# Two-layer mixer with mixture-of-experts: the first experts' biases as two-part float32r rows, and their gate applied to the experts' rows

## The chip, the cores and the metric

The kernel runs on one core of a Trainium2 chip. The metric is the device time of one execution in microseconds (us); lower is better. The time before is 2146.15 us, the median of three runs (2144.57 to 2146.51).

## The reference, cut to what matters

The program is two whole blocks, one after the other, over 256 tokens of width 1024 in float32. Only the feed-forward part of the first block is touched: 32 experts, of which every token uses four.

```python
def moe_ffn(h, w_router, b_router, w_gate_up, b_gate_up, w_down, b_down):
    ...
    top_val, top_idx = lax.top_k(logits, TOP_K)          # TOP_K = 4 of 32
    probs = jax.nn.softmax(top_val, axis=-1)
    ...
    def expert_block(args):
        xb, e = args
        gu = xb @ w_gate_up[e] + b_gate_up[e]            # 1024 -> 2048
        x_glu = jnp.minimum(gu[:, 0::2], SWIGLU_LIMIT)
        x_lin = jnp.clip(gu[:, 1::2], -SWIGLU_LIMIT, SWIGLU_LIMIT)
        act = x_glu * jax.nn.sigmoid(SWIGLU_ALPHA * x_glu) * (x_lin + 1)
        return act @ w_down[e] + b_down[e]               # 1024 -> 1024
    ...
    out = jnp.einsum('tk,tkd->td', probs.astype(y_pairs.dtype), y_pairs)
```

The block then adds `gate * out` to the residual `x`, where `gate` is one row of 1024 numbers that comes from the conditioning vector and is the same for all tokens.

## The kernel before, in words

`moe1` computes these experts, one after another, over 64 slots each. For each group of four experts, `gather` picks the tokens' columns with one-hot products into `gT`. Per expert, `expert1a` makes the gate-and-up product: eight weight tiles `w` (128 x 2048 float32, 1024 KB) stream through TensorE against the slots of `gT`. Since there are only 64 slots, the output is folded: the two halves `s` of the columns stand on partitions 0 to 63 and 64 to 127 of two accumulators `gu` (128 x 512), so each product writes 64 rows. The bias is added by more products (`brows`, L1332), and VectorE and ScalarE make `act` from it. `expert1b` transposes `act` (`aT`), spreads the one-hots (`oT`), streams four tiles of the down weights into one folded accumulator `y`, adds its bias, and calls `combine`: `weighted` multiplies `y` by the routing weights and splits the result into two float32r parts (`yhi` on ScalarE, `ylo` on VectorE), eight products with `oT` scatter them back to the 256 tokens (`co`, four accumulators of 128 x 512), and VectorE multiplies each by the gate (`gated`, L1193) and adds it to `x` (L1194).

The lambda `pend` delays `expert1b` of expert e until after `expert1a` of expert e+1, and a scheduler then moves instructions a little on each engine. After expert 11 comes `overflow`, a branch for experts with more than 64 tokens: every engine and the DMA queue pass it together. Nine tiles of expert 12 are issued ahead of it, one into the spare slot and eight into `w2`.

The weights arrive through one DMA queue, issued by SyncE (SP) in the order gate-and-up of e+1, then down of e, at L302, into 14 slots that are used in turn: five of the whole program (`own`), one spare, eight of this stage. An issue waits until TensorE has read the tile that was in its slot. The second block (`block2`) loads its first weights into the five `own` slots.

The bias of expert e enters as a product whose stationary operand is a column of the identity, broadcast: it picks row e of a 32-row table.

```python
nc.tensor.matmul(o, pick(r, j).to_broadcast([32, 64]), brows[r, c:c + 512], start=False, stop=True)
```

Of the kernel before, what the change touches and what calls it, by code (L numbers as in the profile page):

```python
# [7 lines left out]
F32 = mybir.dt.float32  # L8
F32R = mybir.dt.float32r
# [4 lines left out]
OP = mybir.AluOpType  # L14
# [216 lines left out]
class Ker:  # L231
# [65 lines left out]
    def wload(self, src, n=WCOL, slot=None):  # L297
        pool, tag = slot or self.wq[self.wi % len(self.wq)]
        t = pool.tile([128, WCOL], F32, name="w", tag=tag, bufs=None)
        if slot is None:  # L300
            self.wi += 1
        self.nc.sync.dma_start(t[:, :n], src)  # L302
        return t
# [873 lines left out]
        nc.vector.scalar_tensor_tensor(lo, y, w, hi.bitcast(F32), op0=OP.mult, op1=OP.subtract)  # L1177
        return hi, lo

    def combine(self, p, x, y, oT, w, gate, bufs=1):  # L1180

        nc = self.nc
        ys = self.weighted(p, y, w, bufs)
        for b in range(2):
            o = [self.ps("co"), self.ps("co")]
            for i in range(2):
                for s in range(2):
                    nc.tensor.matmul(o[s], oT[64 * s:64 * s + 64, 128 * b:128 * b + 128], ys[i][64 * s:64 * s + 64, :],  # L1188
                                     start=(i == 0), stop=(i == 1))
            for s in range(2):  # L1190
                cs = slice(512 * s, 512 * s + 512)
                part = p.tile([128, 512], F32, name="gated", tag="gated", bufs=1)
                nc.vector.tensor_mul(part, o[s], gate[:, cs])  # L1193
                nc.vector.tensor_add(x[:, b, cs], x[:, b, cs], part)  # L1194

    def spread(self, p, ohv, bufs=1):
# [55 lines left out]
    def expert1a(self, p, g, c0, wload, bias, feed=iter(())):  # L1252

        nc = self.nc
        gu = [self.pg("gu"), self.pg("gu")]
        for k in range(8):
            if k % 2 == 0:
                next(feed, None)
            w = wload(k)
            for j in range(2):  # L1260
                for s in range(2):
                    nc.tensor.matmul(gu[j][64 * s:64 * s + 64, :], g[:, k, c0:c0 + 64],  # L1262
                                     w[:, 1024 * s + 512 * j:1024 * s + 512 * j + 512], start=(k == 0), stop=False)
        for j in range(2):
            for s in range(2):
                bias(gu[j][64 * s:64 * s + 64, :], 0, 1024 * s + 512 * j)
        act = p.tile([128, 512], F32, name="act", tag="act", bufs=2)
        lin = p.tile([128, 512], F32, name="lin", tag="lin", bufs=1)
        sg = p.tile([128, 512], F32, name="sge", tag="sge", bufs=1)
        for j in range(2):  # L1270
            cs = slice(256 * j, 256 * j + 256)
            nc.vector.tensor_scalar(act[:, cs], gu[j][:, 0::2], 7.0, None, op0=OP.min)  # L1272
            nc.vector.tensor_scalar(lin[:, cs], gu[j][:, 1::2], 7.0, -7.0, op0=OP.min, op1=OP.max)
        self.last_sig = nc.scalar.activation(sg, act, AF.Sigmoid, scale=1.702)  # L1274
        nc.vector.tensor_mul(act, act, sg)
        nc.vector.scalar_tensor_tensor(act, lin, 1.0, act, op0=OP.add, op1=OP.mult)
        return act

    def expert1b(self, p, x, act, wload, bias, ohv, wv, gate):
        nc = self.nc  # L1280
        pt = self.ps("aT")
        for j in range(4):
            nc.tensor.transpose(pt[:, 128 * j:128 * j + 128], act[:, 128 * j:128 * j + 128], self.ident)
        aT = p.tile([128, 4, 2, 64], F32, name="aT", tag="aT", bufs=1)
        nc.scalar.copy(aT.rearrange("p j s n -> p (j s n)"), pt)
        oT = self.spread(p, ohv)
        y = self.ps("y")
        for k in range(8):
            if k % 2 == 0:
                w = wload(8 + k // 2)  # L1290
            for s in range(2):
                o = 1024 * (k % 2) + 512 * s
                nc.tensor.matmul(y[64 * s:64 * s + 64, :], aT[:, k % 4, k // 4, :], w[:, o:o + 512], start=(k == 0), stop=False)  # L1293
        for s in range(2):
            bias(y[64 * s:64 * s + 64, :], 1, 512 * s)
        self.combine(p, x, y, oT, wv, gate)

    def moe1(self, p, route, ahead, spare):
        nc, d, tc = self.nc, self.d, self.tc
        A, B = self.Affn, self.mcol1[:, 0, 24:32]  # L1300
        x = self.x1
        sel, cw, r = route

        def fetch(e, j, slot=None):
            if isinstance(e, int):
                gu, dn = d['wgu'][e], d['wdn'][e]
            else:
                gu = d['wgu'][bass.ds(e, 1)].rearrange("e k n -> (e k) n")
                dn = d['wdn'][bass.ds(e, 1)].rearrange("e k n -> (e k) n")
            if j < 8:  # L1310
                return self.wload(gu[128 * j:128 * j + 128, :], slot=slot)
            return self.wload(dn[128 * (j - 8):128 * (j - 8) + 128, :], slot=slot)
        first = {(0, j): fetch(0, j, ahead) for j in range(NW2)}
        self.wi = 0
        brows = p.tile([96, 1024], F32, name="brows")
        for j in range(2):
            nc.sync.dma_start(brows[32 * j:32 * j + 32, :], d['bgu'][:, 1024 * j:1024 * j + 1024])
        nc.sync.dma_start(brows[64:96, :], d['bdn'])
        self.load_gf()
        gtb = p.tile([128, 1024], F32, name="gtb2")  # L1320
        self.bcast_rows([(1, 10), (1, 11)], [gtb[:, 0:512], gtb[:, 512:1024]])
        xs = self.split_tokens(p, x, r)
        pm, cnt = self.slots(p, sel)

        def wl(e):
            return lambda j: first.pop((e, j)) if isinstance(e, int) and (e, j) in first else fetch(e, j)

        def bias_of(pick):
            def bias(o, which, c):
                j, c = (2, c) if which else divmod(c, 1024)  # L1330
                r = slice(32 * j, 32 * j + 32)
                nc.tensor.matmul(o, pick(r, j).to_broadcast([32, 64]), brows[r, c:c + 512], start=False, stop=True)  # L1332
            return bias

        def late(g, c0, i, ohv, w):
            bsel = p.tile([96, 1], F32, name="bsel")
            for j in range(3):
                r = slice(32 * j, 32 * j + 32)
                nc.vector.tensor_copy(bsel[r, :], self.ident[r, 32 * j:32 * j + 32][:, bass.ds(i, 1)])
            bias = bias_of(lambda r, j: bsel[r, 0:1])  # L1340
            self.expert1b(p, x, self.expert1a(p, g, c0, wl(i), bias), wl(i), bias, ohv, w, gtb)
        pend = None
        for e in range(32):
            feed = iter(())
            if e % 4 == 0:
                oh = self.onehots(p, pm, e)
                g, feed = self.gather(p, xs, 4, [oh[:, b].rearrange("p e s -> p (e s)") for b in range(2)], A, B)
                next(feed)
                if pend:
                    pend()  # L1350
                    pend = None
            bias = bias_of(lambda r, j, e=e: self.ident[r, 32 * j + e:32 * j + e + 1])
            act = self.expert1a(p, g, 64 * (e % 4), wl(e), bias, feed)
            if e == 0:
                cw = cw()
            if e % 4 == 0:
                sw = self.slot_weights(p, [(slice(64 * s, 64 * s + 64), j, [oh[:, b, j, :] for b in range(2)],
                                            [cw[:, b, e + j:e + j + 1] for b in range(2)]) for j in range(4) for s in range(2)], "sw", 4)
            if pend:
                pend()  # L1360
            ohv = [oh[:, b, e % 4, :] for b in range(2)]
            pend = lambda act=act, e=e, ohv=ohv, bias=bias, w=sw[:, e % 4:e % 4 + 1]: self.expert1b(p, x, act, wl(e), bias, ohv, w, gtb)
            if e == OVF:
                pend()
                pend = None

                first = {(e + 1, j): fetch(e + 1, j, spare if j < NW2X else ahead) for j in range(NW2 + NW2X)}
                self.overflow(p, cnt, pm, cw, xs, A, B, late)
        pend()
        self.dump('x2', x)  # L1370
# [759 lines left out]
```

## Time and profile before

| | before |
|---|---|
| median of the runs | 2146.15 us |
| the profiled execution, its own time | 2146.77 us |
| its span in the trace | 2144.9 us |
| TensorE (PE) busy | 2007.6 us, 94% |
| VectorE (DVE) busy | 918.6 us, 43% |
| ScalarE (ACT) busy | 529.8 us, 25% |
| HBM read | 642.91 MB, 300 GB/s over the span |
| first experts, first gate-and-up product to last product of `y` | 576 to 1538 us |

An instruction has a start, a duration and, where its engine was idle before it, what ended the idle time. PE is the matrix product, PEld the load of its stationary operand, SPq the issue of a DMA. One float32 product is recorded as two matmuls. "PEclk" is the share of full clock that TensorE was granted: 1.00 is 2.4 GHz, 0.50 is 1.2 GHz.

### The profile page before, as it was taken

How to read it: one execution, taken by the hardware profiler on the slowest of the kernel's cores; microseconds unless marked ns; L12 is line 12 of the kernel's file. 1: busy time of each engine (PE TensorE's matmuls, PEld its weight loads, DVE VectorE, ACT ScalarE, POOL GpSimd, SP SyncE). 2: the span in 40 equal slices, each digit the busy share in tenths (PEclk: the TensorE clock that was granted, in tenths of full speed). 3: DMA queues.
4: the chain of work that ended last, by engine and by line, in shares of the span. 5: the costliest groups of instructions: out<-in, count | busy, mean ns of one | idle time of the engine just before them, and what ended most of it. 6: DMA issues, size and time to landing. Idle time of an engine off the chain costs nothing. (4 is left out here: it accounts for less than half of the span.)

```text
span 2144.9 us, 30936 instructions
## 1 busy us (share of the span) xinstructions
PE 2007.6 (94%) x13008; PEld 1172.9 (55%) x13009; DVE 918.6 (43%) x1766; ACT 529.8 (25%) x927; POOL 63.2 (3%) x66
## 2 busy tenths in 40 slices
PE   5999999999899999989999999999789998899995
PEld 3788888877633333333333333333268997665552
DVE  5766664454323332332423333333477654322223
ACT  3434463444300000000000000010244634312112
POOL 0000000000000000000000000000033101000000
PEclk9999999999999999989999999999899998999998
DMA  9254637622899999889999999999662232799980
GB/s 356 83 228 184 234 128 282 247 90 82 325 426 427 412 427 417 366 360 405 427 427 427 426 427 427 426 427 427 243 239 105 100 135 105 316 387 381 358 337 26
DMA packets 95127, 646.08 MB, mean 301 GB/s; under 512 B 11524, under 2 KB 12548, under 8 KB 19076
## 3 DMA queue, kind: packets, MB, share of 16 engines
q1 hardware_dynamic: 93296, 642.79, 74.0%
q8 instruction: 107, 1.75, 0.3%
q10 hardware_dynamic: 1684, 1.21, 0.2%
q14 instruction: 40, 0.33, 0.0%
HBM read 642.91 MB, written 1.05 MB: 300 GB/s over the span
## 5 line engine op out<-in xcount | busy, mean ns | idle before, releaser
L1262 PE MATMUL gu<-w,gT 128*64 128x512 f32 x2048 | 480.9, 596 | 0.0
L1262 PEld LDWEIGHTS gu<-w,gT 128*64 128x64 f32 x2048 | 148.1, 137 | 277.7 <-issue 255.8
L1293 PE MATMUL y<-w,aT 128*64 128x512 f32 x1024 | 231.0, 604 | 0.4
L487 DVE TENSOR_TENSOR wsl<-w,wsh 128x1024 fp32r<-128x1024 f32 (+1 forms) x141 | 168.5, 1205 | 98.5 <-ACT wsh L486 98.3
L486 ACT CAST wsh<-w 128x1024 fp32r<-128x1024 f32 (+1 forms) x141 | 143.4, 1030 | 167.0 <-PE tp L500 109.2
L1272 DVE TENSOR_SCALAR act<-gu 128x256 f32<-128x256 f32 x64 | 27.2, 424 | 307.2 <-PE gu L1332 303.9
L1177 DVE SCALAR_TENSOR_TENSOR ylo<-y,sw,yhi 128x512 fp32r<-128x512 f32 x64 | 48.1, 751 | 254.7 <-ACT yhi L1176 254.7
L1293 PEld LDWEIGHTS y<-w,aT 128*64 128x64 f32 x1024 | 72.5, 140 | 149.7 <-issue 143.4
L499 PE MATMUL tp<-hs,wsh 128*128 128x256 f32 (+1 forms) x424 | 140.2, 331 | 0.0
L501 PE MATMUL tp<-hs,wsl 128*128 128x256 f32 (+1 forms) x424 | 134.9, 318 | 4.1 <-DVE wsl L487 4.1
L500 PE MATMUL tp<-hs,wsh 128*128 128x256 f32 (+1 forms) x424 | 134.2, 317 | 0.0
L1445 PE MATMUL ab<-w,gT 128*64 128x256 f32 x1024 | 128.0, 383 | 0.1
L1176 ACT ACTIVATE yhi<-y,sw 128x512 fp32r<-128x512 f32 x64 | 44.0, 687 | 294.9 <-PE y L1332 241.9
L1193 DVE TENSOR_TENSOR gated<-co,gtb 128x512 f32<-128x512 f32 x128 | 88.3, 690 | 34.9 <-PE co L1188 27.4
L1274 ACT ACTIVATE sge<-act 128x512 f32<-128x512 f32 x32 | 20.2, 630 | 331.3 <-DVE act L1272 331.3
L1445 PEld LDWEIGHTS ab<-w,gT 128*64 128x64 f32 x1024 | 77.9, 137 | 39.6 <-issue 10.7
L499 PEld LDWEIGHTS tp<-hs,wsh 128*128 128x128 f32 x424 | 82.4, 194 | 16.3 <-issue 4.9
L1218 PE MATMUL ga<-oh,xhi 128*128 128x256 f32 x256 | 75.8, 325 | 15.9 <-DVE cnt L1149 6.9
L1194 DVE TENSOR_TENSOR x<-x,gated 128x512 f32<-128x512 f32 x128 | 88.2, 689 | 3.3
L501 PEld LDWEIGHTS tp<-hs,wsl 128*128 128x128 f32 x424 | 82.2, 194 | 9.8 <-DVE wsl L487 4.7
L499 PE MATMUL tp<-hi,wsh 128*128 128x256 f32 x288 | 85.5, 297 | 0.0
L500 PEld LDWEIGHTS tp<-hs,wsh 128*128 128x128 f32 x424 | 82.3, 194 | 4.5 <-issue 0.7
(548 smaller groups left out, 3242.1 us busy)
## 6 DMA issues: line engine op xcount, KB each, us to landing
w<-in_wgu_dram SPq DMA_DIRECT2D x256, 1024.0 KB, 13.4
w<-in_wdn_dram SPq DMA_DIRECT2D x128, 1024.0 KB, 14.1
w<-in_win_dram SPq DMA_DIRECT2D x50, 1024.0 KB, 5.8
w<-in_w3e_dram SPq DMA_DIRECT2D x32, 1024.0 KB, 8.8
w<-in_w1e_dram SPq DMA_DIRECT2D x32, 1024.0 KB, 9.2
w<-in_w2e_dram SPq DMA_DIRECT2D x32, 1024.0 KB, 7.6
w<-in_wada_dram SPq DMA_DIRECT2D x24, 1024.0 KB, 6.0
w<-in_wmod_dram SPq DMA_DIRECT2D x16, 1024.0 KB, 5.7
```

The source lines that it names most:

```text
L486: nc.scalar.copy(hi, src)
L487: nc.vector.tensor_sub(lo, src, hi.bitcast(F32))
L499: nc.tensor.matmul(out, a[0], b[0], start=first, stop=False)
L500: nc.tensor.matmul(out, a[0], b[1], start=False, stop=False)
L501: nc.tensor.matmul(out, a[1], b[0], start=False, stop=last)
L1177: nc.vector.scalar_tensor_tensor(lo, y, w, hi.bitcast(F32), op0=OP.mult, op1=OP.subtract)
L1193: nc.vector.tensor_mul(part, o[s], gate[:, cs])
L1194: nc.vector.tensor_add(x[:, b, cs], x[:, b, cs], part)
L1218: nc.tensor.matmul(ps[:, 256 * kk:256 * kk + 64 * n], xs[i][:, b, 128 * (k + kk):128 * (k + kk) + 128], ohv[b], start=(b + i == 0), stop=( ...
L1262: nc.tensor.matmul(gu[j][64 * s:64 * s + 64, :], g[:, k, c0:c0 + 64], w[:, 1024 * s + 512 * j:1024 * s + 512 * j + 512], start=(k == 0), s ...
L1293: nc.tensor.matmul(y[64 * s:64 * s + 64, :], aT[:, k % 4, k // 4, :], w[:, o:o + 512], start=(k == 0), stop=False)
L1445: nc.tensor.matmul(ps[64 * j:64 * j + 64, 256 * i:256 * i + 256], g[:, k, c0 + 64 * j:c0 + 64 * j + 64], w[j][:, k, :], start=(k == 0), st ...
```

## The change

Three things are rewritten, all in the first experts.

1. The biases. Each is split once into two float32r parts, high and low, in a table of 128 rows: high parts of the left half of the columns in rows 0 to 31, low parts in 32 to 63, the same for the right half in 64 to 127 (`bra` for gate-and-up, `brb` for down). A stationary matrix `brow` (128 x 128, made per expert by one VectorE instruction from a block matrix `blk` and a column of `fold`) adds both parts to both halves of an accumulator in one product. So three float32r products over 128 rows (L1357) stand where six float32 products over 32 rows stood.
2. The gate. It depends on the column alone, so it is multiplied into the folded `y` (128 x 512, L1297) before `weighted`, from a folded gate `gtb1`, and not into the four scattered accumulators. `combine` adds `co` to `x` directly.
3. The tables are loaded by 12 small DMAs in place of three, and split by three ScalarE copies and six VectorE subtractions at the first use.

```diff
-    def combine(self, p, x, y, oT, w, gate, bufs=1):
+    def combine(self, p, x, y, oT, w, gate=None, bufs=1):
...
-                part = p.tile([128, 512], F32, name="gated", tag="gated", bufs=1)
-                nc.vector.tensor_mul(part, o[s], gate[:, cs])
+                part = o[s]
+                if gate is not None:
+                    part = p.tile([128, 512], F32, name="gated", tag="gated", bufs=1)
+                    nc.vector.tensor_mul(part, o[s], gate[:, cs])
                 nc.vector.tensor_add(x[:, b, cs], x[:, b, cs], part)
...
         for j in range(2):
-            for s in range(2):
-                bias(gu[j][64 * s:64 * s + 64, :], 0, 1024 * s + 512 * j)
+            bias(gu[j], 0, 512 * j)
...
-        for s in range(2):
-            bias(y[64 * s:64 * s + 64, :], 1, 512 * s)
-        self.combine(p, x, y, oT, wv, gate)
+        bias(y, 1, 0)
+        part = p.tile([128, 512], F32, name="gated", tag="gated", bufs=1)
+        nc.vector.tensor_mul(part, y, gate)
+        self.combine(p, x, part, oT, wv)
...
-        brows = p.tile([96, 1024], F32, name="brows")
-        for j in range(2):
-            nc.sync.dma_start(brows[32 * j:32 * j + 32, :], d['bgu'][:, 1024 * j:1024 * j + 1024])
-        nc.sync.dma_start(brows[64:96, :], d['bdn'])
+        brow = [p.tile([128, n], F32R, name=m) for n, m in ((1024, "bra"), (512, "brb"))]
+        raw = []
+        for t, src, n in ((brow[0], d['bgu'], 1024), (brow[1], d['bdn'], 512)):
+            for c in range(0, n, 512):
+                raw.append((t[:, c:c + 512], p.tile([128, 512], F32, name="braw", tag=("lin", "sge", "ylo")[len(raw)])))
+                for i in range(4):
+                    nc.sync.dma_start(raw[-1][1][32 * i:32 * i + 32, :], src[:, n * (i // 2) + c:n * (i // 2) + c + 512])
...
+        def bias_parts():
+            while raw:
+                t, st = raw.pop(0)
+                nc.scalar.copy(t, st)
+                for r in (slice(32, 64), slice(96, 128)):
+                    nc.vector.tensor_sub(t[r, :], st[r, :], t[r, :].bitcast(F32))
...
-        def bias_of(pick):
-            def bias(o, which, c):
-                j, c = (2, c) if which else divmod(c, 1024)
-                r = slice(32 * j, 32 * j + 32)
-                nc.tensor.matmul(o, pick(r, j).to_broadcast([32, 64]), brows[r, c:c + 512], start=False, stop=True)
+        def bias_of(one):
+            rows = p.tile([128, 128], F32R, name="brow", tag="brow", bufs=2)
+            nc.vector.tensor_scalar(rows, blk, one, None, op0=OP.mult)
+            def bias(o, which, c):
+                bias_parts()
+                nc.tensor.matmul(o, rows, brow[which][:, c:c + 512], start=False, stop=True)
             return bias
```

The order of TensorE's instructions for experts 9 and 10, before: `gu` are gate-and-up products, `gu<-brows` and `y<-brows` the biases, `co` the scatter of expert 9, and the first `gu` of expert 11 is moved between `y` and `co`.

```order
L1262 MATMUL gu<-w,gT 64x512 x24
L1332 MATMUL gu<-brows,fc 64x512 x4
L1293 MATMUL y<-w,aT 64x512 x16
L1332 MATMUL y<-brows,fc 64x512 x2
L1262 MATMUL gu<-w,gT 64x512
L1188 MATMUL co<-yhi,oT 128x512 x2
L1188 MATMUL co<-ylo,oT 128x512 x2
L1188 MATMUL co<-yhi,oT 128x512 x2
L1188 MATMUL co<-ylo,oT 128x512 x2
L1262 MATMUL gu<-w,gT 64x512 x7
```

and at the same place in the changed kernel:

```order
L1294 MATMUL y<-w,aT 64x512 x16
L1357 MATMUL y<-brb,brow 128x512
L1264 MATMUL gu<-w,gT 64x512
L1188 MATMUL co<-yhi,oT 128x512 x2
L1188 MATMUL co<-ylo,oT 128x512 x2
L1188 MATMUL co<-yhi,oT 128x512 x2
L1188 MATMUL co<-ylo,oT 128x512 x2
L1264 MATMUL gu<-w,gT 64x512 x7
```

Four and two bias products became two and one; what stands between `y` and `co` is one gate-and-up product in both.

The order on VectorE from `act` to the end of a `combine`, before (expert 10, ahead of the branch; `gtb_5348` is the gate):

```order
L1276 SCALAR_TENSOR_TENSOR act<-lin,act 128x512
L1177 SCALAR_TENSOR_TENSOR ylo<-y,sw,yhi 128x512
L1193 TENSOR_TENSOR gated<-co,gtb_5348 128x512
L1194 TENSOR_TENSOR x<-x,gated 128x512
L1193 TENSOR_TENSOR gated<-co,gtb_5348 128x512
L1194 TENSOR_TENSOR x<-x,gated 128x512
L1193 TENSOR_TENSOR gated<-co,gtb_5348 128x512
L1194 TENSOR_TENSOR x<-x,gated 128x512
```

and in the changed kernel:

```order
L1277 SCALAR_TENSOR_TENSOR act<-lin,act 128x512
L1297 TENSOR_TENSOR gated<-y,gtb_5365 128x512
L1177 SCALAR_TENSOR_TENSOR ylo<-gated,sw,yhi 128x512
L1196 TENSOR_TENSOR x<-x,co 128x512 x4
```

The gate's multiplication moved ahead of `ylo` (and of `yhi`, which reads `gated` too), once per expert; after `co` four additions are left.

## Rows read from the trace of the kernel before

**Rows 1.** Busy time by stretch: three groups of four experts, and one before them.

```profile
core 0: us, PE busy (x) PEld busy (x) DVE busy (x) ACT busy (x) POOL busy (x), PEclk, DMA share, GB/s
576.00:712.50 136.50, 133.92 (x689) 50.26 (x688) 42.27 (x75) 12.64 (x20) 0.00 (x0) 0.99 0.99 409
960.10:1081.70 121.60, 119.00 (x611) 44.09 (x609) 40.71 (x72) 9.76 (x16) 0.00 (x0) 0.97 0.99 417
1081.70:1201.20 119.50, 116.43 (x579) 42.12 (x577) 40.45 (x71) 9.79 (x16) 0.00 (x0) 0.99 1.01 427
1201.20:1320.10 118.90, 115.21 (x578) 40.97 (x576) 40.35 (x71) 9.86 (x16) 0.00 (x0) 1.00 1.01 427
```

**Rows 2.** Busy time by stretch: around the branch, after it, and the stage's last loads.

```profile
900.00:920.00 20.00, 18.36 (x84) 6.08 (x82) 6.15 (x11) 1.90 (x3) 0.00 (x0) 0.93 0.43 174
920.00:980.00 60.00, 52.81 (x272) 22.14 (x272) 16.89 (x33) 4.16 (x8) 0.00 (x0) 0.88 0.92 378
980.00:1510.00 530.00, 516.54 (x2540) 184.42 (x2542) 179.16 (x311) 43.08 (x71) 0.11 (x1) 0.99 1.01 427
1510.00:1515.00 5.00, 5.00 (x24) 1.39 (x22) 0.99 (x3) 0.00 (x0) 0.00 (x0) 1.00 0.72 303
```

**Rows 3.** Timeline of one expert: start us, us, engine, line, operation [idle before <-releaser].

```profile
1005.83 1.93 PE L1332 MATMUL gu<-brows,fc 32*64 32x512 f32 x8
...
1007.69 7.09 PE L1293 MATMUL y<-w,aT 128*64 128x512 f32 x32
...
1014.71 1.07 PE L1332 MATMUL y<-brows,fc 32*64 32x512 f32 x4
...
1015.89 0.69 ACT L1176 ACTIVATE yhi<-y,sw 128x512 fp32r<-128x512 f32 x1 [6.93 <-PE y L1332]
1016.61 0.75 DVE L1177 SCALAR_TENSOR_TENSOR ylo<-y,sw,yhi 128x512 fp32r<-128x512 f32 x1 [6.20 <-ACT yhi L1176]
...
1017.75 0.40 PE L1188 MATMUL co<-yhi,oT 64*128 64x512 f32 x2
...
1017.98 0.40 PE L1188 MATMUL co<-ylo,oT 64*128 64x512 f32 x2
...
1018.31 3.65 PE L1262 MATMUL gu<-w,gT 128*64 128x512 f32 x14
```

**Rows 4.** The tile `gated`: durations ns min/median/max, and who waited for it.

```profile
L1193 DVE TENSOR_TENSOR gated<-co,gtb x128: 679/692/693, 623.6 to 1545.0; 128x512 f32<-128x512 f32 x128
...
  PEld ga L1218: 13.7, 18
  PEld aT L1283: 13.4, 18
```

**Rows 5.** Timeline around the branch (DMA issues are SPq).

```profile
893.81 0.33 SPq L302 DMA_DIRECT2D w<-in_wdn_dram  x1
...
914.17 13.90 SPq L302 DMA_DIRECT2D w<-in_wgu_dram  x8
...
929.35 1.07 PE L1332 MATMUL y<-brows,fc 32*64 32x512 f32 x4
...
932.53 0.69 DVE L1193 TENSOR_TENSOR gated<-co,gtb 128x512 f32<-128x512 f32 x1 [0.59 <-PE co L1188]
...
937.82 0.69 DVE L1194 TENSOR_TENSOR x<-x,gated 128x512 f32<-128x512 f32 x1
939.22 0.55 PE L1218 MATMUL ga<-oh,xhi 128*128 128x256 f32 x1 [6.26 <-DVEq L1232]
...
940.54 0.34 SPq L302 DMA_DIRECT2D w<-in_wgu_dram  x1
```

**Rows 6.** Timeline of the stage's end: experts 30 and 31.

```profile
1499.70 2.04 SPq L302 DMA_DIRECT2D w<-in_wdn_dram  x2
...
1521.67 1.07 PE L1332 MATMUL y<-brows,fc 32*64 32x512 f32 x4
...
1528.47 8.55 PE L1293 MATMUL y<-w,aT 128*64 128x512 f32 x32
...
1536.95 1.07 PE L1332 MATMUL y<-brows,fc 32*64 32x512 f32 x4
...
1545.76 0.69 DVE L1194 TENSOR_TENSOR x<-x,gated 128x512 f32<-128x512 f32 x1
```

More of the change, by code (lines that the diff above doesn't have):

```diff
@@ L1314, in moe1 @@
         self.wi = 0
-        brows = p.tile([96, 1024], F32, name="brows")
-        for j in range(2):
-            nc.sync.dma_start(brows[32 * j:32 * j + 32, :], d['bgu'][:, 1024 * j:1024 * j + 1024])
-        nc.sync.dma_start(brows[64:96, :], d['bdn'])
-        self.load_gf()
-        gtb = p.tile([128, 1024], F32, name="gtb2")
-        self.bcast_rows([(1, 10), (1, 11)], [gtb[:, 0:512], gtb[:, 512:1024]])
+        brow = [p.tile([128, n], F32R, name=m) for n, m in ((1024, "bra"), (512, "brb"))]
[5 more added lines that the diff above has]
+                    nc.sync.dma_start(raw[-1][1][32 * i:32 * i + 32, :], src[:, n * (i // 2) + c:n * (i // 2) + c + 512])
+        blk = p.tile([128, 128], F32, name="blk")
+        nc.vector.memset(blk, 0.0)
+        for s in range(2):
+            nc.vector.memset(blk[64 * s:64 * s + 64, 64 * s:64 * s + 64], 1.0)
+        def bias_parts():
[4 more added lines that the diff above has]
+                    nc.vector.tensor_sub(t[r, :], st[r, :], t[r, :].bitcast(F32))
+        self.load_gf()
+        gtb = p.tile([128, 512], F32, name="gtb1")
+        ps = self.ps("bc")
+        for s in range(2):
+            row = self.msrc(1, 10 + s)[1]
+            nc.tensor.matmul(ps[64 * s:64 * s + 64, :], self.fold[:, row:row + 1].to_broadcast([128, 64]), self.rowall, start=True, stop=True)
+        nc.scalar.copy(gtb, ps)
         xs = self.split_tokens(p, x, r)
@@ L1326, in wl @@
             return lambda j: first.pop((e, j)) if isinstance(e, int) and (e, j) in first else fetch(e, j)
-        def bias_of(pick):
+        def bias_of(one):
+            rows = p.tile([128, 128], F32R, name="brow", tag="brow", bufs=2)
+            nc.vector.tensor_scalar(rows, blk, one, None, op0=OP.mult)
             def bias(o, which, c):
-                j, c = (2, c) if which else divmod(c, 1024)
-                r = slice(32 * j, 32 * j + 32)
-                nc.tensor.matmul(o, pick(r, j).to_broadcast([32, 64]), brows[r, c:c + 512], start=False, stop=True)
+                bias_parts()
+                nc.tensor.matmul(o, rows, brow[which][:, c:c + 512], start=False, stop=True)
             return bias
         def late(g, c0, i, ohv, w):
[L1336 to L1340, printed above, removed]
+            bsel = p.tile([128, 1], F32, name="bsel")
+            nc.vector.tensor_copy(bsel, self.fold[:, bass.ds(i, 1)])
+            bias = bias_of(bsel)
             self.expert1b(p, x, self.expert1a(p, g, c0, wl(i), bias), wl(i), bias, ohv, w, gtb)
@@ L1351, in moe1 @@
                     pend = None
-            bias = bias_of(lambda r, j, e=e: self.ident[r, 32 * j + e:32 * j + e + 1])
+            bias = bias_of(self.fold[:, e:e + 1])
             act = self.expert1a(p, g, 64 * (e % 4), wl(e), bias, feed)
```

## The prediction

> **What bounds the kernel now.** I read the stretches first. In three regular groups of four experts [rows 1] the reader is to see two full engines at once: PE is busy 115 to 119 us of 119 to 122, and the DMA engines have a share of 0.99 to 1.01 at 417 to 427 GB/s. A group loads 48 tiles of 1024 KB (1.049 MB). At 427 GB/s a tile takes 2.456 us and a group 117.9 us; the second and third group took 119.5 and 118.9. So TensorE sets the pace, but only 1.0 to 1.6 us per group above what the loads need: whatever TensorE saves beyond that is not had in these groups.
>
> The Trainium skill, DMA: Bandwidth & Descriptors, Specifications, gives a core about 358 GB/s from HBM. By it a tile would take 2.93 us and a group 141 us (an estimate); the groups took 119 to 122, so the trace disagrees and the 427 of the rows is used.
>
> Then I looked for stretches where the loads do not run [rows 2]. Around the branch after expert 11 there are holes: 174 GB/s for 20 us lacks 11.8 us of full rate, 378 GB/s for 60 us lacks 6.9, together 18.7. After that the rate is 427 for 530 us. At 1510 to 1515, 303 GB/s is 3.5 us of full rate, so the last down tile lands at about 1513.5.
>
> The timeline around the branch [rows 5] says why: the last down tile of expert 11 is issued at 893.81, the next issue comes at 914.17, when TensorE has read the tiles of y(10), and the queue goes on behind the branch only at 940.54. Of the 8.15 us of full rate in 900 to 920 [rows 2] some 4.2 follow that issue, so the queue was empty from about 903.9. TensorE is late, not the loads. The end [rows 6] shows the same lateness: the last tile landed at 1513.5, but y(31) gets its bias only at 1536.95 and the last addition to x ends at 1546.5. That is 23 us of landed work still to be done.
>
> So the kernel has two floors close together, and TensorE's backlog behind the loads is paid twice, at the branch and at the end. That backlog, not the steady pace, is what a faster expert can give back.
>
> **The change part by part.**
>
> Gate-and-up bias. Now 1005.83 to 1007.69, 1.86 us [rows 3]. After: two float32r products of 512 columns. The nearest row is `co`, where a float32r product of 512 columns on both halves of the rows starts 0.23 us after the one before (1017.75, 1017.98). Two are 0.46, plus some 0.1 for the change of shape: I take 1.3 us saved per expert, on TensorE's path. Bounds: 1.4 (no change of shape), and 0.1 if the new product ran at the float32 pace, 0.88 each (y's sixteen, two at a time, take 7.02).
>
> From y's end to the next gate-and-up. Now 1014.71 to 1018.31, 3.60 us: bias 1.07, hop 0.11, `yhi` 0.69, hop 0.03, then 1.70 from the start of `ylo` to the restart [rows 3]. After: product 0.45, hop 0.11, gate 0.69 [rows 4], hop 0.1, `yhi` 0.69, hop 0.03, 1.70: 3.77. The added serial instruction takes back the whole saving of the bias and 0.15 more. Queued behind it on TensorE: the eight `co` and everything after, since only one gate-and-up product stands between. Bounds: -0.4 (ScalarE reads SBUF faster) to +0.8 (the product as slow as today's bias).
>
> Four gate multiplications less per `combine`, 0.69 each. On VectorE they are hidden: it is busy 40 of 119.5 us. What shows is that accumulators come free later now: PEld waited for `gated` 13.7 and 13.4 us over 18 times each [rows 4], 0.75 per time, mostly at group boundaries. Bounds 0 to 3.4 us per group (27.1 over eight); I take 1.0, since a first accumulator comes free no earlier than now.
>
> Per group TensorE saves 4 x 1.15 + 1.0 = 5.6 us, 119.5 to about 114, below the 117.9 of the loads. From there the loads bind.
>
> At no cost: `brow`, one VectorE instruction per expert, at most 0.69, beside the same idle VectorE. The split at the start: three ScalarE copies and six subtractions, at most 3 x 0.69 + 6 x 0.75 = 6.6 us, beside the first expert's products; without that cover it would delay the first bias by as much. Twelve small loads in place of three, 0.79 MB against 0.39: 1 us of the queue, ahead of the stage, nine issues more at 0.33 [rows 5] on SP's queue: 3 us, before its tiles for expert 0 go on. Taken as 0, bound 4.
>
> Branch. Twelve experts and three boundaries save 12 x 1.15 + 3 = 16.8: y(11)'s bias moves from 929.35 to 912.5, and y(10)'s last tile is read at 914.17 - 15.7 = 898.5. That is before the queue runs dry at 903.9, so the first hole closes. From the start of y(11)'s bias to the last addition takes 9.16 us now (929.35 to 938.51) [rows 5]. After: 0.45 + 0.11 + 0.69 + 0.1 + 0.69 + 0.03 + 0.75 + 0.59 and four additions, 3.0: 6.4. The branch opens at 918.9, SP goes on 2.0 later as now, 920.9. The nine tiles ahead keep the queue busy from 903.9 for 22.1 us, to 926. The second hole closes too. A third, some 2 to 5 us when expert 12's slots come free, may stay. So 18.7 of hole becomes 0 to 5; I take 3.
>
> End. The last tile lands at 1513.5 - 16 = 1497.5. TensorE alone would reach y(31)'s bias 597.7 - 20 x 1.15 - 5 = 569.7 after its restart at 919.6: 1489, earlier, so the loads decide. y(30)'s last tile lands 9.8 before the end, its four products take 1.7, from its bias to y(31) are 6.8 (1521.67 to 1528.47), y(31) takes 7.1 to 8.5: its bias at 1497.5 - 8.1 + 6.9 + 7.1 = 1503.4. Now 1536.95: 33.5 saved. The tail is 3.1 shorter (9.5 to 6.4). Sum 36.6, and 1 to 2 more where the loads now lose a little in the first groups (409 GB/s in the first stretch [rows 1]): 38 us.
>
> The profiled execution took 2146.77 us, 0.6 over the median of 2146.15. 2146.8 - 38 = **2108 us** (against the median the same within its spread).
>
> **Rivals.**
>
> *The hole stays open in part.* If TensorE saves only 0.6 per expert, y(10) is read at 907.6, the queue is dry for 5 us, y(11)'s bias comes at 922.2, TensorE goes on at 929.3 and, not the loads, sets the end: 929.3 + 597.7 - 12 = 1515, 22 saved plus 3: 2122. For it: the serial gate; against: the 1.86 us bias is plain. 10%.
>
> *Block 2 cannot take it up.* Its first tiles go into the five own slots, which come free with y(30) and y(31). Five tiles are 12.3 us of the queue; now they land behind y(31), after the change right behind the last down tile. If its first two rows of modulation had to wait for four of them, some 8 us are lost: 2116. Against: each is issued when its slot is read, as now, and the queue has nothing else left by then. 8%.
>
> *The loads are not the floor.* Then y(31)'s bias is at 1489: 2146.8 - 48 - 3 = 2096. It would take a queue above the 427 GB/s that no stretch of the rows exceeds. 2%.
>
> *The change doesn't do what it says:* the float32r product over 128 rows runs at the float32 pace. Then 0.1 is saved and 0.8 lost: TensorE is 0.7 slower per expert, 32 x 0.7 = 22, less 8 at the boundaries and the shorter tail twice, 6: 2155. Against: `co`. 3%.
>
> *Slower by the clock.* The change lengthens TensorE's idle time ahead of `co` in every expert by 0.8 us. In the groups where the granted clock averaged 0.97 and 0.99 rather than 1.00, in places behind two `combine`s close together, the group took 121.6 and 119.5 against 118.9 [rows 1]: a fall to 1.2 GHz costs 0.6 to 2.7 us. If it came after each of 32 `combine`s at 2.7, less some 10 that are paid today, that is 76 against 45 saved on TensorE: +31, less the shorter tail twice, 6: 2172. It decides from 1.4 us per expert on. For it: clock 0.88 around the branch [rows 2]. Against: four `combine`s with the same kind of gap passed at 1.00 in the last group, and TensorE has 3.9 us of slack per group before it matters. 4%.
>
> The Trainium skill, TensorE: Matmul & The Clock Gate, A second HAM failure mode, says that short idle times between groups of products, when accumulators are cycled, can make the clock swing. That rule speaks against this change; by it 2172. The trace has it at boundaries alone so far.
>
> **How the numbers follow.** The forecast has 73%, 2101 to 2116 by the bounds of the third hole (3), of the boundaries and the start (4); the first two rivals 18%, up to 2122 and a little over; loads not the floor 2%; slower 7%. The range is 2099 to 2125. No change can be told from one within 0.2%, 4.3 us. Faster 0.92; same 0.02 (a clock that falls now and then); slower 0.06.
>
> **What would show it.** In the changed profile: the regular groups at 117.9 to 118.5 with 427 GB/s, now with PE waiting for `w` often; no stretch under 400 GB/s from 900 to 940; branch passed near 920; `yhi` waiting for `gated`, 0.8 later behind y; y(31)'s product near 1503 and within 7 us of the last landing; the stage's end 37 us earlier and everything behind it shifted by as much. Wrong if groups take 119 or more (a product or a clock slower than taken), if a hole stays at 900 to 915, or if block 2 waits for its first tiles.

## The result, and the profile after

| | before | after |
|---|---|---|
| median of the runs | 2145.59 us (four runs) | 2118.53 us (four runs, 2116.62 to 2122.73) |
| ratio | | 0.9875 (0.9862 to 0.9888) |
| the profiled execution, its own time | 2146.77 us | 2116.62 us |
| its span | 2144.9 us | 2114.9 us |
| TensorE busy | 2007.6 us | 1950.4 us |
| VectorE busy | 918.6 us | 855.7 us |

The kernel is 27 us faster by the medians and 30 by the two traces; 38 was forecast. The range held the result; the forecast's own case, 2101 to 2116, just missed it. I read the same places as before.

The stretches, with the columns of [rows 1], answer to [rows 1, 2]: three groups of four experts, the branch, and all loads behind it.

```profile
1031.90:1150.90 119.00, 110.73 (x543) 42.65 (x541) 32.29 (x63) 10.00 (x16) 0.00 (x0) 0.99 1.01 427
1150.90:1270.00 119.10, 110.70 (x542) 42.71 (x540) 32.28 (x63) 10.00 (x16) 0.00 (x0) 0.99 1.01 427
1270.00:1389.10 119.10, 110.15 (x542) 42.92 (x540) 31.63 (x61) 10.00 (x16) 0.00 (x0) 0.99 1.01 427
900.00:920.00 20.00, 11.69 (x61) 4.42 (x61) 8.79 (x15) 2.03 (x3) 0.00 (x0) 0.95 1.00 415
920.00:930.00 10.00, 8.19 (x42) 5.42 (x42) 1.57 (x4) 1.13 (x2) 0.00 (x0) 0.76 0.61 231
930.00:1500.00 570.00, 533.39 (x2632) 204.72 (x2633) 154.45 (x301) 49.27 (x78) 0.00 (x0) 0.99 1.01 427
```

PE is busy 110 us of 119 in a group, where it was 115 to 119 of 119 to 122, and the queue runs at 427 GB/s there and from 930 to 1500. TensorE's saving shows as idle time. Around the branch the holes lack 0.6 us (900 to 920) and 4.6 us (920 to 930) of full rate, 5.2 where 18.7 were.

What SP waited for in three groups (us in total, times, longest) says who holds the loads: first the kernel before, 1059 to 1417 us, then the changed one, 1032 to 1389.

```profile
SPq L302 <- PE gu L1262: 175.2, 90, 6.7
SPq L302 <- PE y L1293: 74.8, 41, 7.3
SPq L302 <- DMA w<-in_wgu_dram: 25.0, 19, 2.1
SPq L302 <- DMA w<-in_wdn_dram: 16.2, 12, 2.1
```

```profile
SPq L302 <- DMA w<-in_wgu_dram: 199.3, 96, 3.5
SPq L302 <- DMA w<-in_wdn_dram: 100.2, 48, 3.5
SPq L302 <- PE gu L1264: 2.6, 11, 0.3
...
SPq L302 <- PE y L1294: 1.8, 6, 0.4
```

Before, SP waited 250 us for TensorE to read a tile and 41 for transfers under way; now 300 for transfers and 4 for tiles to be read. The slots come free ahead of the queue.

One expert, as [rows 3]:

```profile
984.04 0.73 PE L1357 MATMUL gu<-bra,brow 128*128 128x512 f32 x2
984.70 7.09 PE L1294 MATMUL y<-w,aT 128*64 128x512 f32 x32
991.72 0.50 PE L1357 MATMUL y<-brb,brow 128*128 128x512 f32 x1
...
992.26 0.69 DVE L1297 TENSOR_TENSOR gated<-y,gtb 128x512 f32<-128x512 f32 x1 [4.42 <-PE y L1357]
...
993.05 0.72 ACT L1176 ACTIVATE yhi<-gated,sw 128x512 fp32r<-128x512 f32 x1 [6.65 <-DVE gated L1297]
...
993.82 0.50 PE L1188 MATMUL co<-yhi,oT 64*128 64x512 f32 x2 [0.60 <-ACT yhi L1176]
...
995.50 3.65 PE L1264 MATMUL gu<-w,gT 128*64 128x512 f32 x14
```

The gate-and-up bias takes 0.66 us (984.04 to 984.70) where it took 1.86, and `yhi` starts 0.79 behind `gated`. From y's bias to the next gate-and-up run are 3.78 us, where 3.60 were.

The branch, as [rows 5], and the stage's end, as [rows 6]:

```profile
899.51 11.18 SPq L302 DMA_DIRECT2D w<-in_wgu_dram  x8
...
911.97 0.50 PE L1357 MATMUL y<-brb,brow 128*128 128x512 f32 x1
912.08 0.33 SPq L302 DMA_DIRECT2D w<-in_wdn_dram  x1
...
915.38 2.48 DVE L1196 TENSOR_TENSOR x<-x,co 128x512 f32<-128x512 f32 x4 [0.58 <-PE co L1188]
...
1490.31 1.94 PE L1294 MATMUL y<-w,aT 128*64 128x512 f32 x8 [0.51 <-DMA w<-in_wdn_dram]
...
1492.18 0.50 PE L1357 MATMUL y<-brb,brow 128*128 128x512 f32 x1
...
1504.74 0.50 PE L1357 MATMUL y<-brb,brow 128*128 128x512 f32 x1
...
1508.16 2.48 DVE L1196 TENSOR_TENSOR x<-x,co 128x512 f32<-128x512 f32 x4 [0.59 <-PE co L1188]
```

y(31)'s bias comes 32.2 us earlier than in [rows 6], and the last addition to x ends at 1510.6, 35.8 earlier. The program ends only 30.0 earlier. What gives 6 us back lies behind the first experts, in the opening of the second block.

There TensorE has three kinds of work: `modps` (rows of modulation), `pw` and `pg` (small products that wait for `xm` from VectorE, one step after another), and `tp` (the projections). First the changed kernel's timeline of PE from 1521, with rows left out between:

```profile
1521.07 1.97 PE L1632 MATMUL xT<-fc,xh 128*128 128x128 f32 x8 [7.04 <-DVE xh L1604]
...
1528.44 1.12 PE L1680 MATMUL pw<-xm,lora 128*64 128x256 f32 x2 [1.14 <-DVE xm L1676]
...
1533.67 1.11 PE L1680 MATMUL pw<-xm,lora 128*64 128x256 f32 x2 [2.00 <-DVE xm L1676]
...
1546.39 0.39 PE L499 MATMUL tp<-hi,wsh 128*128 128x256 f32 x1
```

and at the same place in the kernel before:

```profile
1559.26 0.87 PE L1609 MATMUL xT<-fc,xh 128*128 128x128 f32 x3 [14.74 <-DVE xh L1581]
...
1570.72 0.70 PE L1659 MATMUL pg<-xm,lora 128*128 128x256 f32 x2
1571.07 0.47 PE L499 MATMUL tp<-hi,wsh 128*128 128x256 f32 x1
```

From the first `xT` (PE's transpose of `xh`) to the first `tp` are 25.3 us; in the kernel before they are 11.8. The program's text is the same there. The kernel before runs one step of `pw` and `pg`, eight `modps`, one more step, then fifteen `tp` between each two steps; the changed kernel has six steps of `pw` and `pg` ahead of the first `tp`. The scheduler put them there.

The Trainium skill, TensorE: Matmul & The Clock Gate, Step-by-step: what each phase is for, says that TensorE runs its matmuls in program order and pulls only the loads of stationary operands ahead. The trace agrees: `tp` stands behind the 2.00 us wait for `xm`, and begins after the last of the six steps.

### The profile page after: what moved, and what is told of

It reads as the page before. It is cut to its first block, busy times and chain, and to the rows that moved or that the text cites. A ratio compares the mean times of both kernels' runs of the same rounds, so it can differ in the third digit from the quotient of the medians.

```text
span 2114.9 us, 30238 instructions
## 1 busy us (share of the span) xinstructions
PE 1950.4 (92%) x12720; PEld 1168.2 (55%) x12721; DVE 855.7 (40%) x1711; ACT 532.3 (25%) x929; POOL 60.8 (3%) x66
## 5 line engine op out<-in xcount | busy, mean ns | idle before, releaser
L1264 PEld LDWEIGHTS gu<-w,gT 128*64 128x64 f32 x2048 | 158.0, 137 | 253.9 <-issue 236.9
L1297 DVE TENSOR_TENSOR gated<-y,gtb 128x512 f32<-128x512 f32 x32 | 22.1, 692 | 171.6 <-PE y L1357 171.6
L499 PEld LDWEIGHTS tp<-hs,wsh 128*128 128x128 f32 x424 | 81.7, 193 | 16.3 <-issue 4.9
L1196 DVE TENSOR_TENSOR x<-x,co 128x512 f32<-128x512 f32 x128 | 79.4, 682 | 18.9 <-PE co L1188 18.9
L1176 ACT ACTIVATE yhi<-gated,sw 128x512 fp32r<-128x512 f32 x32 | 23.1, 721 | 238.9 <-DVE gated L1297 238.9
L1220 PEld LDWEIGHTS ga<-oh,xhi 128*128 128x128 f32 x256 | 53.1, 207 | 53.0 <-issue 32.2
```

The lines of the kernel that those rows point to most:

```text
L499: nc.tensor.matmul(out, a[0], b[0], start=first, stop=False)
L1176: nc.scalar.activation(hi, y, AF.Identity, scale=w)
L1220: nc.tensor.matmul(ps[:, 256 * kk:256 * kk + 64 * n], xs[i][:, b, 128 * (k + kk):128 * (k + kk) + 128], ohv[b], start=(b + i == 0), stop=( ...
```

## The experiments

My theory after these readings: (1) the biases free TensorE, and behind the branch the loads are the floor; (2) the moved gate is worth little by itself; (3) the second block's new order gives some 6 us back. Rivals stand with each run. Times are medians; where start times decide, they are collected in a table at the end.

**One half each.** `bias_only` has the changed kernel's biases and the old `combine`; `gate_only` is the kernel before with the gate on `y`.

```diff
 # bias_only, against the changed kernel (the gate's table as before; not shown)
-        part = p.tile([128, 512], F32, name="gated", tag="gated", bufs=1)
-        nc.vector.tensor_mul(part, y, gate)
-        self.combine(p, x, part, oT, wv)
+        self.combine(p, x, y, oT, wv, gate)
 # gate_only, against the kernel before (with the changed combine and gate table; not shown)
-        self.combine(p, x, y, oT, wv, gate)
+        part = p.tile([128, 512], F32, name="gated", tag="gated", bufs=1)
+        nc.vector.tensor_mul(part, y, gate)
+        self.combine(p, x, part, oT, wv)
```

> The changed biases alone; the gate stays in combine, on the four scattered accumulators. Theory (the loads are the floor of the groups behind the branch, and TensorE's saving comes from the biases): 2112 to 2122 us, as the full change within 4 us, since every expert saves the 2 us of its two biases without the serial gate instruction (about 0.7), and the later accumulators cost no more than that. Rival (the gate's move carries the saving, by accumulators that come free earlier): 2128 to 2138 us. From the load-bound groups 119.0 us each is expected in both.

Measured: 2118.75 us, ratio 0.9877 (0.9856 to 0.9898), the same as the full change. y(31)'s bias stands at 1505.3, where the full change has 1504.7. The biases alone carry the gain in the first experts.

> The moved gate alone, with the old biases in six products. Theory: no gain by itself; the serial gate instruction adds 0.7 to 0.8 us between the last product of y and the next gate-and-up product in each of 32 experts, and the accumulators that come free earlier return 1 to 3 us per group: 2143 to 2158 us. Rival (the shorter combine is what made the kernel faster): 2125 to 2137 us.

Measured: 2153.52 us, ratio 1.0038 (1.0024 to 1.0051). The time is in the theory's range, but not for its reason: y(31)'s bias came at 1534.3, 2.7 us earlier than before. Inside the experts the accumulators that come free earlier pay for the serial gate; the loss lies behind them.

**Are the loads the floor?** Eleven of twelve tiles per expert are loaded, while TensorE does every product.

```diff
-            w = wload(k)
+            if k < 7:
+                w = wload(k)
```

> The changed kernel with one of twelve weight tiles per expert not loaded: the eighth gate-and-up tile is left out and the seventh is multiplied in its place, so that part of the computation is changed, while TensorE does all its products. Theory (loads set the pace behind the branch): groups of 119.0 us fall to about 115, the product of y(31) comes some 13 us earlier, 2100 to 2108 us. Rival (TensorE sets the pace and the loads merely keep it company): 2115 to 2119 us.

Measured: 2098.85 us, 19.7 less than the full change and a little more gain than the theory's 2100 to 2108. Two of its groups, with the columns of [rows 1]:

```profile
1141.40:1255.60 114.20, 109.33 (x543) 41.28 (x541) 32.26 (x63) 10.00 (x16) 0.00 (x0) 0.99 1.01 426
1255.60:1369.70 114.10, 109.31 (x543) 41.30 (x541) 31.59 (x61) 10.00 (x16) 0.00 (x0) 0.99 1.00 407
```

114.1 us is what TensorE takes where no tile is late (PE waits for no `w` there); the group before these took 113.0. The loads therefore cost the full change about 5 of its 119.1 us. y(31)'s bias came 23.0 us earlier; I had written 13.

> The kernel before with the same tile left out (the eighth gate-and-up tile of each expert is not loaded, the seventh is used twice). Theory (TensorE set the pace before, the loads only 1 to 1.6 us per group under it): 2139 to 2147 us. Rival (before, the loads set the pace too): 2115 to 2130 us.

Measured: 2140.61 us, ratio 0.9978 (0.9966 to 0.999). Its groups took 117.8 to 118.6 where the kernel before took 118.9 and 119.5 [rows 1]. With the old biases TensorE set the pace, and the loads cost about 1 us per group.

**The order of the second block.** `pinned` holds `pw` and `pg` behind the product ahead of them in the program (`last_mm` is set at the modulation and `tp` products):

```diff
-            nc.tensor.matmul(pw[0:64, :256], lora1[k][:, 0:64], xs[0], **f)
-            nc.tensor.matmul(pw[64:128, :256], lora1[k][:, 64:128], xs[1], **f)
-            nc.tensor.matmul(pg[:, :256], lora1[k][:, 128:256], xs[2], **f)
+            with tc.issue_after(self.last_mm.ins):
+                nc.tensor.matmul(pw[0:64, :256], lora1[k][:, 0:64], xs[0], **f)
+                nc.tensor.matmul(pw[64:128, :256], lora1[k][:, 64:128], xs[1], **f)
+                nc.tensor.matmul(pg[:, :256], lora1[k][:, 128:256], xs[2], **f)
```

> The changed kernel with one thing more: in the second block's opening the small products pw and pg are held behind the modulation product that precedes them in the program, so that the scheduler cannot move a row of them ahead of the transposing products tp. Theory (about 6 us of what the first experts saved are given back in block 2's opening because the scheduler put the pw and pg products of six steps, which wait for weight tiles, ahead of tp): 2110 to 2115 us, and the lag behind the kernel before is 35 us or more at the first tp product. Rival (the loads, or TensorE at 1.2 GHz, delay the opening whatever the order): 2117 to 2121 us.

Measured: 2112.63 us, ratio 0.9848 (0.9835 to 0.9861). PE's timeline at the same place:

```profile
1520.35 1.97 PE L1632 MATMUL xT<-fc,xh 128*128 128x128 f32 x8 [7.16 <-DVE xh L1604]
...
1530.32 1.07 PE L358 MATMUL modps<-w,cpad 128*32 128x512 f32 x8
1531.32 0.38 PE L499 MATMUL tp<-hi,wsh 128*128 128x256 f32 x1
```

No wait for `xm` is left, and `tp` starts 11.0 us behind `xT`. The theory stands, on the full change, in its main point; what the moved products wait for is `xm`, not weight tiles as I had written.

What the order costs is read from `xT` to P, the first product that waits for `bh`, some 65 us into the block. First the changed kernel, then `pinned`, with the columns of [rows 1]:

```profile
1521.07:1595.62 74.55, 65.25 (x412) 46.89 (x412) 55.40 (x86) 34.99 (x50) 25.55 (x25) 0.88 0.50 187
1520.35:1587.25 66.90, 60.60 (x412) 46.19 (x412) 55.29 (x86) 35.10 (x50) 26.87 (x25) 0.93 0.55 209
```

Of the 7.6 us between them, 3.0 are idle time of PE (its waits for `xm` are 3.1), and 4.6 are the same 412 matmuls taking longer: the granted clock is 0.50 from `xT` until 1539 in the changed kernel and until 1528 in `pinned`, and 1.00 from there to 1595 and 1586. So the rival's slow clock is part of the price, but the order decides how long it lasts.

> The changed kernel once more, on the same chip and in the same rounds as e12_pinned_again. Theory (the second block's order costs 4 to 8 us) and rival (the 6 us between e5_pinned and the changed kernel came from the runs being on different chips) both: 2116 to 2121 us. In the trace: the first tp product about 25 us after the first xT product.

> The changed kernel with pw and pg held, the kernel of e5_pinned, beside e11_after_again. Theory: 4 to 8 us faster than e11_after_again, first tp product 11 us after the first xT product. Rival: within 2 us of e11_after_again, whatever tp does, because the time is given back at the next wait, as in e8_bias_pinned.

Measured on the same chip in the same rounds: 2118.2 (2115.9 to 2122.6) and 2114.17 us (2113.6 to 2114.5), ratios 0.9879 and 0.9855. Holding is worth 4 us here, the lower end of what the theory said, and `pinned` is faster than both kernels in each comparison. Why 4 and not 7.6 is told in the last section.

**Does holding help the halves?** The same edit on `bias_only`, on `gate_only` and on the kernel before.

> The changed biases alone (gate in combine), with the second block's pw and pg products held in place as in e5_pinned. Theory (the two biases make nearly the whole gain in the first experts, and the scheduler's new order of the second block's opening takes 4 to 6 us back in every version that shortens an expert's chain): 2112 to 2116 us. Rival (the moved gate is worth another 3 us, the four multiplications less in the tail behind y(31)): 2116 us and more, where e5_pinned took 2112.6.

Measured: 2119.73 us, ratio 0.9876 (0.9859 to 0.9892), as without the hold. The theory fails here: `tp` came 4.8 us earlier than in `bias_only`, and the end 2.3 later. Part of it is not the hold's: y(31)'s bias was 1.6 later in this execution. Counted from there, P comes 2.9 us sooner with the hold, and from P to the end 3.6 us more are lost, 1.2 of them right behind P (18.8 us up to the first `tt` product, where `bias_only` takes 17.5). So the new order is not the only term in this block. The time is where the rival had it (2116 and more), and the moved gate does have a share: from y(31) to P this kernel needs 88 us, `pinned` 83.

> The moved gate alone (old biases), with the second block's pw and pg products held in place as in e5_pinned. Theory (e2_gate_only was slower through the second block's opening alone: its y(31) came 2.7 us earlier than in the kernel before, its end 6.8 later): 2140 to 2145 us. Rival (the serial gate instruction costs the experts 0.7 us each, and what e2_gate_only lost, it lost there): 2150 to 2156 us.

Measured: 2149.47 us, ratio 1.0015 (1.0005 to 1.0025): 4 us of the 8 that `gate_only` lost come back, not all. The rest shows in PE's waits from 1600 to 1700, and in a stretch of 10 us (the last three columns are PEclk, DMA share and GB/s):

```profile
PE yk L1910 <- issue: 2.0, 1, 2.0
```

```profile
1645.00:1655.00 10.00, 8.11 (x68) 5.72 (x69) 3.15 (x6) 2.33 (x5) 2.94 (x5) 0.66 0.01 2
```

At 1646.9 PE waits 2.0 us for nothing that the profile shows, and the granted clock in the 10 us around it is 0.66 on average, part of it at 1.2 GHz. `gate_only` has the same gap at 1651.1. Between 1620 and 1680 the held kernel loses 5.5 us against the kernel before and `gate_only` 5.9 (by the starts of the same instructions); neither the kernel before nor the changed one has the gap. Why it comes with this half alone is open.

> The kernel before with the same pw and pg products held in place: a control. Its order in the second block's opening is the old one already. Theory (holding is worth something only where the scheduler has moved these products): 2143 to 2148 us, as the kernel before. Rival (holding is a gain by itself, for any kernel): 2138 to 2141 us.

Measured: 2146.09 us, ratio 1.0003 (0.9993 to 1.0012). Holding is no gain where nothing was moved.

**The branch.** `no_branch` leaves the call of `overflow` out.

```diff
-                self.overflow(p, cnt, pm, cw, xs, A, B, late)
```

> The changed kernel without the branch after expert 11 (it leaves out the path for experts with more than 64 tokens). Theory (the branch costs SyncE 14.7 us between two DMA issues, and the queue runs dry for 4.7 us): the hole goes, the last tile lands 4 to 6 us earlier, 2111 to 2115 us. Rival (the hole is made up for later): 2117 to 2120 us.

Measured: 2118.81 us, ratio 0.9875 (0.986 to 0.989), as the full change. Neither side was tested, because the hole did not go. SP's issues around it, the first gate-and-up products of expert 12, and SP's longest wait from 912 to 945:

```profile
915.05 0.33 SPq L302 DMA_DIRECT2D w<-in_wdn_dram  x1
...
922.61 3.65 PE L1264 MATMUL gu<-w,gT 128*64 128x512 f32 x16
...
926.30 9.99 SPq L302 DMA_DIRECT2D w<-in_wgu_dram  x8
```

```profile
SPq L302 <- PE gu L1264: 17.9, 5, 10.8
```

Without the branch SP goes on at 926.30, with it at 926.73. It now waits 10.8 us, until TensorE has read the first two tiles of expert 12 (922.61 + 3.65). But this wait was made by the edit. The last line of `overflow` also sets the slot counter `wi` back to 0:

```python
self.last_sig, self.wq, self.wi = sig, wq, 0
```

With the call, the loads behind the branch begin with the five `own` slots, whose tiles TensorE had read by y(10) (899.4 in the changed kernel). Without it the counter goes on from the 136 loads ahead, to the eleventh of the 14 slots: one of the eight that were just filled with expert 12. What the branch costs the queue is therefore open; a run without it that keeps the reset was not made.

**A second serial pass.** `gate_twice` multiplies the gated rows by 1.0 once more.

```diff
         nc.vector.tensor_mul(part, y, gate)
+        nc.vector.tensor_scalar(part, part, 1.0, None, op0=OP.mult)
```

> The changed kernel with one more pass of VectorE over the gated rows (times 1.0) in the serial chain of every expert, about 0.7 us. Theory (TensorE sets the pace up to the branch, the loads behind it, with 3.5 to 4 us of slack per group): the twelve experts before the branch delay it by 8 to 9 us, which the queue loses whole, and the twenty behind it cost almost nothing: 2124 to 2130 us. Rival (the serial chain sets the pace everywhere): 32 times 0.7, 2140 to 2144 us. Second rival (loads alone set the pace, the branch included): 2118 to 2121 us.

Measured: 2126.69 us (2119.0 to 2127.9), ratio 0.9911 (0.9896 to 0.9926). The median is in the theory's range, but the run does not show its reason. The extra pass is shorter than planned (min/median/max in ns):

```profile
L1297 DVE TENSOR_TENSOR gated<-y,gtb x32: 691/692/693, 616.8 to 1504.4; 128x512 f32<-128x512 f32 x32
L1298 DVE TENSOR_SCALAR gated<-gated x32: 417/420/428, 617.6 to 1505.2; 128x512 f32<-128x512 f32 x32
```

The scheduler also put three gate-and-up products in place of one between y and `co`, so the chain is covered otherwise. And the profiled execution is the one of 2119.0 us, with y(11)'s bias at 910.4, no later than in the full change. Where the other three lost 7 to 9 us no trace shows; their mean granted clock is 0.962 to 0.965, and 0.968 in the profiled one. Inconclusive.

The start times behind these readings, in us of each trace:

| kernel | y(31) bias | first xT | first tp | P | span |
|---|---|---|---|---|---|
| before | 1537.0 | 1559.3 | 1571.1 | 1624.4 | 2144.9 |
| before, held | 1536.3 | 1558.6 | 1570.4 | 1623.8 | 2144.4 |
| gate_only | 1534.3 | 1551.4 | 1572.8 | 1624.0 | 2151.7 |
| gate_only, held | 1535.7 | 1552.8 | 1564.3 | 1620.2 | 2147.4 |
| bias_only | 1505.3 | 1527.0 | 1543.7 | 1596.1 | 2115.9 |
| bias_only, held | 1506.9 | 1528.6 | 1538.9 | 1594.8 | 2118.2 |
| after | 1504.7 | 1521.1 | 1546.4 | 1595.6 | 2114.9 |
| after, again | 1504.3 | 1520.6 | 1546.0 | 1595.2 | 2114.6 |
| pinned | 1504.0 | 1520.4 | 1531.3 | 1587.3 | 2110.9 |
| pinned, again | 1504.6 | 1520.9 | 1531.9 | 1587.9 | 2111.8 |

From y(31) to xT the old `combine` takes 21.7 to 22.3 us and the moved gate 16.3 to 17.1. From xT to P the order before takes 65; the scheduler's new order 69 with the biases alone, 73 with the gate alone and 75 with both; held, 66 to 67. Those two stretches nearly cancel between the full change and `bias_only`, which is why the two are equal: the 5 to 6 us that the gate's move saves up to xT pay for the worse order. From P to the end the traces lie between 519 and 528 us.

## Why the prediction was right, and where it was wrong

The result lies in the stated range, but not by the forecast's own case, which ended at 2116: the range reached 2125 for two rivals that did not come in the form given. Step by step, the forecast of 38 us and the 30 of the traces compare so:

| step | forecast | measured |
|---|---|---|
| y(31)'s bias earlier | 33.5 | 32.2 |
| from it to the end of the last addition to x | 3.1 | 3.6 |
| from there to xT | 0 | 2.4 |
| a little more from the first groups | 1 to 2 | none apart |
| opening of the second block, xT to P | 0 | -9.4 |
| P to the end | 0 | 1.2 |

**Gate-and-up bias.** 0.56 us forecast, 0.66 measured; y's end to the next gate-and-up 3.77 against 3.78. `co` was the right nearest row for the float32r product, and the rival that it runs at float32 pace is out. The lower bound of the second term did not come either: `yhi` took 0.72 us from SBUF (993.05) where it took 0.69 [rows 3].

**Two floors.** Right in kind: TensorE at 113.0 to 114.2 us where it does not wait, shown by leaving tiles out, and loads as the pace behind the branch. That the prediction's 114 came out is in part luck. Its saving of 5.6 us per group was taken from 119.5, which held about 1 us of loads; with the tile left out of both kernels, groups go from 117.8 to 118.6 down to 113.0 to 114.2, 4.5 us on average. Four times the 1.0 us of the two rows above (1.20 saved, 0.18 lost) is 4.1 of it, so the term of 1.0 us for the group boundary was too large. And the groups took 119.0 to 119.1, not 117.9 to 118.5, which the prediction had named as a sign of being wrong. The reasons it gave, a product or a clock slower than taken, are not it: without late tiles TensorE needs 5 us less, and in `bias_only`, held, two groups (1163.9 to 1282.8 and to 1402.0) took 118.9 and 119.2 at a granted clock of 1.00 and 426 to 427 GB/s. What that microsecond is stays open. The row of the Trainium skill that the prediction quotes (DMA: Bandwidth & Descriptors, Specifications) gives its 358 GB/s as half of a stack's 716, for two cores; this program runs on one, so the 427 here does not speak against it.

**Four multiplications less.** The gate's move is worth little inside the experts (`gate_only` reached y(31) 2.7 us earlier, held 1.3). From y(31)'s bias to xT 6.0 us were gained, but only 3.6 of them by the shorter VectorE work up to the last addition, where 3.1 were forecast. The other 2.4 go with an order as well, which was not tried by itself. VectorE's rows behind the last addition, in the kernel before and in the changed one:

```profile
1551.57 1.22 DVE L487 TENSOR_TENSOR wsl<-w,wsh 128x1024 fp32r<-128x1024 f32 x1 [1.75 <-ACT wsh L486]
...
1556.74 3.60 DVE L1581 TENSOR_SCALAR xh<-xh,r 128x1024 f32<-128x1024 f32 x2 [1.78 <-POOL x L1580]
```

```profile
1518.56 3.11 DVE L1604 TENSOR_SCALAR xh<-xh,r 128x1024 f32<-128x1024 f32 x2 [2.23 <-POOL x L1603]
...
1521.79 2.35 DVE L487 TENSOR_TENSOR wsl<-w,wsh 128x1024 fp32r<-128x1024 f32 x2
```

In the kernel before (and in `bias_only`) the splits `wsh` and `wsl` of the second block's weights stand ahead of `xh`, which PE waits for, and in the changed kernel behind it (in `gate_only` one split stands between its two halves). `xh` starts 10.3 us behind the last addition before, 7.9 after.

**Branch.** y(10)'s tile was read at 899.5 (forecast 898.5) and y(11)'s bias came at 912.0 (912.5; at 913.1 to 913.8 in three further traces with the same first experts), so the first hole closed as reasoned. The step that failed here is "SP goes on 2.0 later as now": after the last addition (917.9) TensorE went on at 921.8 and SP at 926.7, not 920.9. The holes lack 5.2 us where I took 3, just past the bounds of 0 to 5, and its sign "no stretch under 400 GB/s from 900 to 940" failed with 231 from 920 to 930. The shorter tail did not bring SP forward: it goes on 8.8 us behind the last addition, 14.8 behind y(11)'s bias, where it was 11.2. What holds it there is not shown, since the run without the branch also moved the slots.

**End.** y(30)'s last tile was used at 1490.3, 2.6 us later than the 1487.7 worked out, and y(31)'s bias came at 1504.7 against 1503.4.

**What failed.** The step of the forecast is "everything behind it shifted by as much". I had costed the rest of the program at the durations of the trace before, as if its order were fixed. It is not: the second block's opening, with the same text, was put in another order, and each half of the change moved steps of waiting products ahead of `tp`: four with the biases alone, five and part of a sixth with the gate alone, six with both, where the kernel before has two. In the full change that costs 7.6 us up to P (74.5 against 66.9 held), 3.0 in idle time and 4.6 at the lower clock, of which 4 to 6 show in the time. My rival "block 2 cannot take it up" had the size (2116) and the place, with another mechanism: it had the first tiles late (PE waits for none from xT to P), and here it is an order. That both halves moved the order is shown; why the scheduler did it is not.

**Clock.** The rival did not come. Granted clock in the regular groups is 0.99 (0.97 to 1.00 before), with TensorE idle 0.60 us ahead of `co` of an inner expert (993.82). The Trainium skill, TensorE: Matmul & The Clock Gate, A second HAM failure mode, speaks of short idle times between groups of products that make the clock swing; at these gaps no run here shows it.

## What to carry to other kernels

When a stage is shortened, the stage behind it moves as a block only if its instruction order stays: compare the new order of every engine to the end of the program, not only where the edit is. Where two floors lie within a few per cent, price the saving against the second floor, and test which one holds by taking load away from each. An experiment that takes a call away takes all that the call does: here a reset of the slot counter went with the branch, and a run that reads as "no effect" says nothing of the branch.

## What had not been expected

SP spends 14.7 us between its issues at the branch (912.08 to 926.73), and what that costs stays open. The half that only moves a multiplication lost 5.5 to 5.9 us some 110 us behind the stage, at a gap of 2.0 us in TensorE's own stream that the profile gives no cause for.

And the time right behind P follows TensorE's clock. From P to the first `tt` product the same 240 matmuls run in every kernel, with PE busy all the time. The changed kernel, `pinned`, and the changed kernel with a tile left out, in which nothing is held (columns of [rows 1]):

```profile
1595.62:1612.99 17.37, 17.37 (x240) 15.84 (x241) 15.55 (x31) 2.68 (x3) 0.00 (x0) 0.90 0.34 123
1587.25:1608.85 21.60, 21.60 (x241) 19.90 (x241) 15.55 (x31) 2.68 (x3) 0.00 (x0) 0.71 0.29 99
1572.47:1594.53 22.06, 22.06 (x241) 20.28 (x241) 15.55 (x31) 2.67 (x3) 0.00 (x0) 0.69 0.27 97
```

They take 17.4 us at a granted clock of 0.90, 21.6 at 0.71 and 22.1 at 0.69; the kernel before takes 18.7 at 0.84 and `bias_only`, held, 18.8 at 0.83. So `pinned` gives back here 4.2 of the 7.6 us that it has gained up to P, in both of its traces. Holding is not the reason by itself: the unheld kernel with a tile less loses as much, the held `bias_only` does not. PE waits about 3 us for `bh` ahead of P in all of them; why the clock stays low longer in some is not shown. From the first `tt` to the end the changed kernel and `pinned` take 501.9 and 502.0 us.
